# Branch A's engines in an order written by hand, three places for gate results, kept sums asked for later, and one sum of the early feed-forward moved ahead of weight sums

## The chip, the cores and the metric

One Trainium2 chip, of which the kernel uses one core. TensorE (PE, with PEld for its weight loads), VectorE (DVE), ScalarE (ACT) and GpSimd (POOL) each work through a queue of their own, in the order in which instructions stand in it; SyncE (SP) issues the DMAs, in the order of its queue. The metric is the device time of one execution in microseconds; a kernel's time is the median of its runs.

## The reference, cut to what matters

A hybrid encoder block over 1024 tokens and 16 meta tokens, width 1024, in float32: differential attention with 4 heads (branch A), windowed grouped attention (branch B), a sigmoid gate for each branch, an output projection, then a SwiGLU feed-forward of width 2816.

```python
def diff_attn_rows(q1, q2, k1, k2, v, qpos, kpos, key_real, slopes, lam):
    ...
    s1 = jnp.einsum('bqhd,bkhd->bhqk', q1, k1).astype(jnp.float32) * scale + bias
    s2 = jnp.einsum('bqhd,bkhd->bhqk', q2, k2).astype(jnp.float32) * scale + bias
    attn = jax.nn.softmax(s1, axis=-1) - lam * jax.nn.softmax(s2, axis=-1)
    return jnp.einsum('bhqk,bkhe->bqhe', attn.astype(v.dtype), v)

def mixer_block(...):
    ...
    merged = jax.nn.sigmoid(ga) * (y_a @ w_ba) + jax.nn.sigmoid(gb) * (y_b @ w_bb)
    return merged @ w_o

def swiglu(h, w_gate, w_up, w_down):
    return (jax.nn.silu(h @ w_gate) * (h @ w_up)) @ w_down
```

## The kernel before

Every large product runs as three products of split operands: a float32 operand is kept as a high part (rounded, written by ACT) and a low part (the difference, written by DVE or POOL), and high x high, high x low and low x high are summed in PSUM. The gates and the feed-forward also use a seven-product scheme on 2 x 2 blocks (products numbered 1 to 7), so that sums of weights and sums of activations are operands, and results of products are sums that are kept and added to later.

The program runs through these stages: the input projection and branch B's attention; **branch A with the gate products** (lines L738 to L893); the two branches' output weights (PE line L808, tiles ppa); the output projection; the feed-forward's gate and up products (L1466, tiles pg), whose first products are the "early feed-forward"; the down products (L1582).

**Branch A** goes through 4 heads of 8 query tiles each, 32 tiles, one round of the loop for each, and one round more, since tile n is scored while tile n-1 is transposed. The string `SLOTS` says in which order PE gets its work in a round: "s" is one block of scores (two matmuls of L829 into a bank, six blocks: three key blocks for softmax 1, then three for softmax 0), "g" one quarter of a gate product (three matmuls of L738), "t" one set of transposes of the tile before (L855), "n" a piece of values or of the head's norm (L868, L881, L891). Only PE's order is fixed by hand in the kernel before (`manual_schedule` for PE); ACT, DVE, POOL and SP have theirs set by the compiler's scheduler, which simulates a timeline.

For one tile, DVE takes each block of scores out of its bank and adds the distance bias with a running minimum (L832, six times), ACT takes the exponential of each softmax's row (L837, twice), DVE inverts the sum (L839), multiplies (L841) and joins the two softmaxes (L843, one pass over 1040 columns, "the join" below, with a short copy L844). PE transposes the joined tile in three pieces (L855); each piece leaves its bank as a high part by ACT (L858) and a low part by DVE (L859). Scores and transposes share five banks (`SC`).

The **gate products** fill PE between these blocks. `g_ahead` loads weights (L620) and splits them ahead (gop, hi by ACT, lo by POOL, L113 and L114). When a gate product's bank is complete, its result is either copied out by ACT (gate_stage, L746, two places: `G_BUFS`) or, for products 1, 6 and 7, added by DVE to a sum that was stored earlier and read back (gk, L743; read at L632 when the weights are split). Both are then stored (L747). Sums of w_o (tiles wo and wo_s, L774 to L786) are made by POOL between. The heads' Q and K are read at the head's first round (`load_a1`, `load_a0`), V with them (`load_v`).

**After the last gate product** come the branch B outputs: yb_raw is split into yb (hi by ACT, lo by DVE), w_b's first two weight blocks were read early (raw_w), the third is wbrb (L789).

**The early feed-forward** has DVE's order fixed by hand too. In it, product n is followed by what its results need (L1475 to L1486: a bank's sum with a stored copy, tile copies_p), by low parts of token sums (L1524, tile t, `low_of`), and `prepare()` makes the operands of a later product, for product 6 three sums of weights first (L1247 to L1249, tiles wf and s).

## Time and profile before

| | |
|---|---|
| three runs | 1453.79 us median (1452.72 to 1456.25) |
| the profiled execution's own time | 1453.61 us |
| its span | 1451.8 us |
| mean granted TensorE clock | 0.993 |
| PE from 324.8 to 638.4 us | branch A and the gate products |
| PE from 638.4 to 725.5 us | the branches' output weights |
| PE from 725.5 to 808.5 us | the output projection |
| PE from 808.5 to 1234 us | feed-forward, gate and up |
| PE from 1234 to 1444.8 us | feed-forward, down |

The columns of the views quoted below: a timeline row has start, duration, engine, line, operation, output<-inputs, shapes, the count of equal instructions in a row, and in brackets how long the engine had been idle before it and what released it. A row of windows has the stretch and its length, then busy time (and instructions) of PE, PEld, DVE, ACT and POOL, the granted clock, the DMA share and GB/s. A row of waits has the waiting line, what it waited for, the total, the number of times and the longest. A row of groups has the count, busy time, the mean in ns, and the idle time ahead of the group's instructions with its releasers.

### The profile page before, as it was taken

How to read it: one execution, taken by the hardware profiler on the slowest of the kernel's cores; microseconds unless marked ns; L12 is line 12 of the kernel's file. 1: busy time of each engine (PE TensorE's matmuls, PEld its weight loads, DVE VectorE, ACT ScalarE, POOL GpSimd, SP SyncE). 2: the span in 40 equal slices, each digit the busy share in tenths (PEclk: the TensorE clock that was granted, in tenths of full speed). 3: DMA queues.
4: the chain of work that ended last, by engine and by line, in shares of the span. 5: the costliest groups of instructions: out<-in, count | busy, mean ns of one | idle time of the engine just before them, and what ended most of it. 6: DMA issues, size and time to landing. Idle time of an engine off the chain costs nothing. (4 is left out here: it accounts for less than half of the span.)

```text
span 1451.8 us, 21189 instructions
## 1 busy us (share of the span) xinstructions
PE 1419.5 (98%) x7231; PEld 1216.4 (84%) x7231; DVE 943.4 (65%) x1680; ACT 696.0 (48%) x1315; POOL 627.2 (43%) x593
## 2 busy tenths in 40 slices
PE   8999999998999899999999999999999999999997
PEld 7998989987888889888888878888888888888886
DVE  7478535637778788733876896554455554787567
ACT  6366535545555455555445633333333333444454
POOL 4599126743532122245144565454445452000444
PEclk9999999999999999999999999999999999999999
DMA  8467668988768564569522624333333333964443
GB/s 242 88 210 239 191 164 269 277 287 290 250 221 257 175 196 155 167 209 330 201 80 88 189 87 150 119 109 105 100 96 107 103 103 105 316 223 139 124 130 139
DMA packets 195804, 255.00 MB, mean 176 GB/s; under 512 B 18976, under 2 KB 116704, under 8 KB 195696
## 3 DMA queue, kind: packets, MB, share of 16 engines
q1 hardware_dynamic: 195696, 253.65, 55.6%
q8 instruction: 57, 0.93, 0.3%
q14 instruction: 51, 0.42, 0.1%
HBM read 165.84 MB, written 81.20 MB: 170 GB/s over the span
## 5 line engine op out<-in xcount | busy, mean ns | idle before, releaser
L114 POOL TENSOR_TENSOR wop<-wf,wop 128x512 fp32r<-128x512 f32 x128 | 175.1, 1372 | 167.8 <-ACT wop L113 155.3
L1466 PE MATMUL pg<-t,wop 128*128 128x512 f32 x1056 | 242.6, 389 | 0.0
L1466 PEld LDWEIGHTS pg<-t,wop 128*128 128x128 f32 x1056 | 198.3, 188 | 41.1
L1582 PE MATMUL pd<-ob,oa 128*128 128x512 f32 x924 | 210.4, 389 | 0.5 <-POOL oa L114 0.4
L1582 PEld LDWEIGHTS pd<-ob,oa 128*128 128x128 f32 x924 | 173.2, 188 | 37.6 <-POOL oa L114 0.9
L1466 PE MATMUL pg<-b,wop 128*128 128x512 f32 x792 | 185.2, 392 | 2.8 <-DVE copies_p L1480 2.8
L1466 PEld LDWEIGHTS pg<-b,wop 128*128 128x128 f32 x792 | 149.5, 189 | 34.2 <-DVE copies_p L1480 3.2
L738 PE MATMUL pg<-hT_hi,gop 128*128 128x512 f32 x384 | 144.4, 400 | 0.4 <-DVE gk L743 0.4
L114 POOL TENSOR_TENSOR gop<-gr,gop 128x512 fp32r<-128x512 f32 x47 | 64.4, 1373 | 165.7 <-ACT gop L113 161.3
L113 ACT ACTIVATE wop<-wf 128x512 fp32r<-128x512 f32 x128 | 80.1, 631 | 84.1 <-PE pg L1466 48.0
L114 POOL TENSOR_TENSOR oa<-ra,oa 128x512 fp32r<-128x512 f32 x33 | 44.1, 1337 | 170.6 <-ACT oa L113 169.2
L113 ACT ACTIVATE oa<-ra 128x512 fp32r<-128x512 f32 x77 | 48.7, 632 | 105.1 <-PE pd L1582 44.0
L837 ACT ACTIVATE as<-as,amn 128x1040 f32<-128x1040 f32 x64 | 74.5, 1164 | 49.9 <-DVE amn L832 41.4
L829 PE MATMUL aps<-ak,aq 128*128 128x392 f32 (+1 forms) x384 | 91.0, 331 | 7.1 <-DVE amn L832 6.2
L1247 DVE TENSOR_TENSOR s<-wf,wf 128x512 f32<-128x512 f32 x22 | 22.3, 1011 | 103.4 <-DMA wf<-in_w_ff_up_dram 52.3
L829 PEld LDWEIGHTS aps<-ak,aq 128*128 128x128 f32 x384 | 70.4, 192 | 21.0 <-DVE amn L832 7.5
L738 PEld LDWEIGHTS pg<-hT_hi,gop 128*128 128x128 f32 x384 | 73.3, 191 | 12.2 <-DVE gk L743 1.1
L339 POOL TENSOR_SCALAR bs<-bs,bdn 128x432 f32<-128x432 f32 (+1 forms) x64 | 41.4, 664 | 86.6 <-DVE bdn L337 74.3
L738 PE MATMUL pg<-hT_lo,gop 128*128 128x512 f32 x192 | 76.5, 398 | 0.0
L114 POOL TENSOR_TENSOR woh<-wo,woh 128x512 fp32r<-128x512 f32 x28 | 38.5, 1378 | 67.4 <-ACT woh L113 66.3
L329 DVE CUSTOM_DVE_ANT_0 bs<-bps,tbx,nsink 128x432 f32<-128x432 f32 (+1 forms) x64 | 38.2, 622 | 38.5 <-PE bps L327 29.3
L832 DVE CUSTOM_DVE_ANT_0 as<-aps,dist,far_a 128x392 f32<-128x392 f32 x64 | 39.6, 619 | 30.2 <-PE aps L829 29.7
(311 smaller groups left out, 3219.2 us busy)
## 6 DMA issues: line engine op xcount, KB each, us to landing
ra<-aop SPq DMA_DIRECT2D x77, 256.0 KB, 2.7
wf<-in_w_ff_gate_dram SPq DMA_DIRECT2D x24, 512.0 KB, 4.0
wf<-in_w_ff_up_dram SPq DMA_DIRECT2D x24, 512.0 KB, 3.9
aop<-as SPq DMA_DIRECT2D x44, 256.0 KB, 2.1
w_c<-in_w_in_dram SPq DMA_DIRECT2D x17, 512.0 KB, 5.9
aop<-c SPq DMA_DIRECT2D x33, 256.0 KB, 2.0
ts_d<-to SPq DMA_DIRECT2D x16, 512.0 KB, 3.6
gw<-in_w_in_dram SPq DMA_DIRECT2D x32, 256.0 KB, 4.2
```

The lines of the kernel that those rows point to most:

```text
L113: nc.scalar.activation(hi, src, AF.Copy)
L114: lo_eng.tensor_tensor(lo, src, f32(hi), ALU.subtract)
L329: nc.vector.tensor_tensor_reduce(st[:, r, :W], ps[:, :W], tb, 2.0 ** -(4 * g + r + 1), nsink[:, 4 * g + r:4 * g + r + 1], ALU.add, ALU.min ...
L339: nc.gpsimd.tensor_scalar(st[:, r, :W], st[:, r, :W], dn[:, r:r + 1], 1.0, ALU.mult, ALU.mult)
L738: nc.tensor.matmul(ps, op[:, a, c], quad(b, *act)[:, c], start=(p in (2, 5, 1) and c == 0 and i == 0), stop=(p in (2, 3, 4) and c == 3 and ...
L829: nc.tensor.matmul(ps[:, :n], qs[m][:, t * P:(t + 1) * P], ks[m][:, vv, k0:k0 + n], start=(vv == 0), stop=(vv == 1))
L832: nc.vector.tensor_tensor_reduce(s[m][:, k0:k0 + n], ps[:, :n], far_by, slope, low, ALU.add, ALU.min, mn[:, m, i:i + 1])
L837: nc.scalar.activation(s[m][:, 0:L], s[m][:, 0:L], AF.Exp, bias=low, scale=-1.0, accum_out=sum_of[m])
L1247: tt(s1, a21, a22, ALU.add)
L1466: nc.tensor.matmul(ps, op[:, x, c, :], b[:, y, c, :], start=(p in (1, 2, 5) and c == 0 and n == 0), stop=(p in (4, 2, 3) and c == 3 and n ...
L1582: nc.tensor.matmul(ps[u], oa[:, a, u * P:(u + 1) * P], ob[:, b, :], start=(p in (1, 2, 5) and j == 0 and k == 0), stop=(p in (2, 3, 4) and ...
```

## The change

Six things change, five of them in branch A:

- ACT, DVE, POOL and SP get an order by hand over the whole loop of branch A. For that, `scores_a` is cut into the blocks themselves and `exp_a`, `scale_a`, `join_a`, which the loop calls at set places: the exponential of softmax 1 and the scale in the same round after the third and fifth block, the exponential of softmax 0 in the next round after the first set of transposes (`EXP_AT`), the join behind the next tile's first block (`JOIN_AT`). Weight splits are held back (`held_back`) and let go at two places of a round, or when a gate product needs them. A round's order for PE stays but for round 1, which gets two more "g" ("sgsgsngsgssggtntnt").
- A gate result is taken out not behind its own last matmul but after the next quarter's three matmuls (`owed`, `gate_result`).
- Gate results have three places instead of two, in another pool; the first uses a place of tag "w". yg has one buffer instead of two.
- Kept sums are no longer read when the weights are split but up to three ahead, at the second quarter of a gate product (`kept_to_do`, `load_kept`), which puts the read behind earlier stores in SP's queue.
- The next head's Q and K are asked for in the last tile of a head, right behind the blocks that used the old ones last; V in the third round of a head; the stores of w_o's sums in the round after they were made. `fill(1000)`, the last gate products, now stands ahead of the closing of the pools.
- In the early feed-forward `prepare()` is left out for products 4 to 7 and called behind product 7, and one of the token sums is made from the other bank's copy (one ACT copy and one DVE subtraction in the place of one DVE subtraction, four times).

```diff
-G_BUFS = 2
+JOIN_AT = 1
+EXP_AT = 1
+G_BUFS = 3
...
         if p in (1, 6, 7):
-            kept = g_kept[p, k] = gpool.tile([P, 512], F32, tag="gk", name=f"gk{p}_{k}", bufs=GK_BUFS)
-            nc.sync.dma_start(kept, g_place(p, k))
+            kept_to_do.append((p, k))
...
+    def load_kept():
+        p, k = kept_to_do.pop(0)
+        kept = g_kept[p, k] = gpool.tile([P, 512], F32, tag="gk", name=f"gk{p}_{k}", bufs=GK_BUFS)
+        nc.sync.dma_start(kept, g_place(p, k))
...
-                what(g_done[i])
+                if i and held_back is not None:
+                    held_back.append(g_done[i])
+                else:
+                    what(g_done[i])
                 g_done[i] += 1
+
+    def let_go(n):
+        while n > 0 and held_back:
+            g_split(held_back.pop(0))
+            n -= 1
...
+    owed = []
+
+    def gate_result(p, k, ps):
+        if p in (1, 6, 7):
+            while (p, k) not in g_kept:
+                load_kept()
+            st = g_kept.pop((p, k))
+            nc.vector.tensor_tensor(st, ps, st, ALU.add)
+        else:
+            tag, bufs = ("w", 2) if (p, k) == order_g[0] else ("g", G_BUFS)
+            st = prepool.tile([P, 512], F32, tag=tag, name=f"gate_stage{p}_{k}", bufs=bufs)
+            nc.scalar.copy(st, ps)
+        nc.sync.dma_start(g_place(p, k), st)
...
             for c in range(4):
...
+                while owed:
+                    gate_result(*owed.pop(0))
+                if c == 1:
+                    while kept_to_do and len(g_kept) < GK_BUFS:
+                        load_kept()
                 if c == 3:
...
+                    owed.append((p, k, ps))
+                    if n == len(order_g) - 1:
+                        gate_result(*owed.pop(0))
                 yield
...
+    order_av = tc.manual_schedule(engines={mybir.EngineType.Activation, mybir.EngineType.DVE, mybir.EngineType.Pool, mybir.EngineType.SP})
+    order_av.__enter__()
     for n in range(AH * NT + T_LAG):
...
-        for what in SLOTS:
-            if what == "s":
-                next(scoring, None)
-            elif what == "t":
-                next(turning, None)
+        if n < AH * NT and t == 2 and h:
+            vs[h] = load_v(h)
+        if n < AH * NT:
+            wo_store()
+            if t in (2, 3, 4, 5):
+                wo_load(4 * h + t - 2)
+        scored = turned = 0
+        if n == AH * NT:
+            join_a(tiles[n - 1][2])
+        for what in SLOTS if n != 1 else "sgsgsngsgssggtntnt":
+            if what == "s" and n < AH * NT:
+                next(scoring)
+                scored += 1
+                if scored == JOIN_AT and n:
+                    join_a(tiles[n - 1][2])
+                if scored == 3:
+                    exp_a(s, 1)
+                    if t == NT - 1 and h < AH - 1:
+                        ahead = load_a1(h + 1)
+                    let_go(1)
+                if scored == 4 and t in (3, 4, 5, 6):
+                    wo_ahead(4 * h + t - 3)
+                if scored == 5:
+                    scale_a(t, s)
+                if scored == 6 and n == 0:
+                    exp_a(s, 0)
+                if scored == 6 and t == NT - 1 and h < AH - 1:
+                    ahead = load_a0(h + 1, *ahead)
+            elif what == "t" and n:
+                next(turning)
+                turned += 1
+                if turned == EXP_AT and n < AH * NT:
+                    exp_a(s, 0)
+                if turned == 3:
+                    let_go(1)
             elif what == "n":
                 step_tail()
-            else:
+            elif what == "g":
                 fill(1)
...
+    order_av.__exit__(None, None, None)
     n_gates[0] += HOLD
     raw_w = []
     while tail:
         step_tail()
+        let_go(9)
         fill(3)
...
     order_pe.__exit__(None, None, None)
+    fill(1000)
     close_pre()
...
-    fill(1000)
     ypool, close_ypool = pool("ypool")
...
-        nc.vector.tensor_tensor(left, t2, left, ALU.subtract)
+        nc.scalar.copy(left, pts[1])
+        nc.vector.tensor_tensor(left, left, pts[0], ALU.subtract)
...
-        if n not in (4, 5):
+        if n not in range(4, 8):
             prepare()
...
         product_f(*steps[n][1])
         used[0] -= 1
+        if n == 7:
+            prepare()
         low_of(2)
```

Three places show how instructions move. The first is ACT's queue around rounds 2 to 4 of branch A: at is the high part of a transposed piece, "as...<-as,amn 128x1040" an exponential (with adn as its sum, it is softmax 1), gop a weight split, gate_stage a gate result. Before:

```order
L837 ACTIVATE as_0_3180,as_0_0_3937<-as_0_3180,amn_2_4064 128x1040
L837 ACTIVATE as_0_3_4141,adn_3_4140<-as_0_3_4141,amn_3_4139 128x1040
L746 COPY gate_stage<-pg_0_4003 128x512
L113 ACTIVATE gop_2_4251<-gr_2_4146 128x512
L858 ACTIVATE at_2_4063<-apt_2_0_4200 128x4x128
L837 ACTIVATE as_1_3181,as_0_0_3937<-as_1_3181,amn_3_4139 128x1040
L858 ACTIVATE at_2_4063<-apt_2_1_4216 128x4x128
L858 ACTIVATE at_2_4063<-apt_2_2_4230 128x128
```

and now:

```order
L115 ACTIVATE gop_3_4147<-gr_3_4038 128x512
L885 ACTIVATE as_0_3_4154,adn_3_4153<-as_0_3_4154,amn_3_4152 128x1040
L756 COPY gate_stage_0_4192<-pg_0_3997 128x512
L909 ACTIVATE at_2_4072<-apt_2_0_4212 128x4x128
L885 ACTIVATE as_1_3181,as_0_0_3934<-as_1_3181,amn_3_4152 128x1040
L909 ACTIVATE at_2_4072<-apt_2_1_4229 128x4x128
L909 ACTIVATE at_2_4072<-apt_2_2_4243 128x128
L115 ACTIVATE gop_2_4247<-gr_2_4104 128x512
L885 ACTIVATE as_0_4_4257,adn_4_4256<-as_0_4_4257,amn_4_4254 128x1040
```

The split stands behind the transposed pieces instead of ahead of them, and softmax 0's exponential always stands between a tile's first and second transposed piece.

The second place is ACT's queue at the end of the gate products: yb is a high part of branch B's output, wbhb of its weights, gate_stage the copies of the last two gate results. Before:

```order
L113 ACTIVATE yb_7340<-yb_raw_6945 128x512
L113 ACTIVATE yb_7341<-yb_raw_6945 128x512
L113 ACTIVATE gop_6_7198<-gr_6_7171 128x512
L113 ACTIVATE gop_7_7228<-gr_7_7196 128x512
L113 ACTIVATE wbhb_7306<-raw_w_7207 128x512
L113 ACTIVATE wbhb_7309<-raw_w_7208 128x512
L746 COPY gate_stage<-pg_6_7084 128x512
L746 COPY gate_stage<-pg_7_7140 128x512
L113 ACTIVATE wbhb_7446<-wbrb_7362 128x512
```

and now:

```order
L115 ACTIVATE gop_6_7221<-gr_6_7171 128x512
L115 ACTIVATE gop_7_7235<-gr_7_7196 128x512
L115 ACTIVATE wbhb_7310<-raw_w_7208 128x512
L115 ACTIVATE wbhb_7313<-raw_w_7209 128x512
L756 COPY gate_stage_6_7285<-pg_6_7065 128x512
L756 COPY gate_stage_7_7298<-pg_7_7133 128x512
L115 ACTIVATE wbhb_7450<-wbrb_7366 128x512
L115 ACTIVATE yb_7342<-yb_raw_6947 128x512
L115 ACTIVATE yb_7343<-yb_raw_6947 128x512
```

The splits of yb, eight in all, stood ahead of the last weight splits and now stand behind the last gate result and behind the third weight block of branch B.

The third is DVE's queue in the early feed-forward: c and copies_p are sums with banks, t low parts of token sums, s and wf sums of weights. Before:

```order
L1475 TENSOR_TENSOR c_1_11_9074<-pg_1_2_9061,copies_p_0_0_8945 128x512
L1524 TENSOR_TENSOR t_8913<-ts_8894,t_8913 128x4x128
L1524 TENSOR_TENSOR t_8912<-ts_8984,t_8912 128x4x128
L1247 TENSOR_TENSOR s_0_0_6_9088<-wf_0_0_9084,wf_0_1_9086 128x512
L1248 TENSOR_TENSOR wf_0_0_9084<-wf_0_0_9084 128x4x128
L1249 TENSOR_TENSOR wf_0_0_9084<-s_0_0_6_9088,wf_0_0_9084 128x4x128
L1247 TENSOR_TENSOR s_1_0_6_9099<-wf_0_0_9095,wf_0_1_9097 128x512
L1248 TENSOR_TENSOR wf_0_0_9095<-wf_0_0_9095 128x4x128
L1249 TENSOR_TENSOR wf_0_0_9095<-s_1_0_6_9099,wf_0_0_9095 128x4x128
L1524 TENSOR_TENSOR t_8912<-ts_9040,t_8912 128x4x128
L1524 TENSOR_TENSOR t_8913<-ts_8984,t_8913 128x4x128
L1480 TENSOR_TENSOR copies_p_0_0_8945<-pg_1_2_9127,copies_p_0_0_8945 128x512
```

and now:

```order
L1552 TENSOR_TENSOR c_1_11_9082<-pg_1_2_9069,copies_p_0_0_8951 128x512
L1601 TENSOR_TENSOR t_8919<-ts_8899,t_8919 128x4x128
L1601 TENSOR_TENSOR t_8918<-ts_8990,t_8918 128x4x128
L1601 TENSOR_TENSOR t_8918<-ts_9047,t_8918 128x4x128
L1601 TENSOR_TENSOR t_8919<-ts_8990,t_8919 128x4x128
L1557 TENSOR_TENSOR copies_p_0_0_8951<-pg_1_2_9107,copies_p_0_0_8951 128x512
L1559 TENSOR_TENSOR c_1_11_9082<-c_1_11_9082,copies_p_0_0_8951 128x512
L1323 TENSOR_TENSOR s_0_0_6_9129<-wf_0_0_9125,wf_0_1_9127 128x512
L1324 TENSOR_TENSOR wf_0_0_9125<-wf_0_0_9125 128x4x128
L1325 TENSOR_TENSOR wf_0_0_9125<-s_0_0_6_9129,wf_0_0_9125 128x4x128
```

The bank's sum (copies_p) and the product with it moved ahead of the six sums of weights; the same count of instructions stands there.

70 lines of the change are left out of this document (35 added, 35 removed).

## The prediction

> **What bounds the kernel now.** First the page: the engines' busy time and shares of the span.
>
> ```profile
> PE 1419.5 (98%) x7231; PEld 1216.4 (84%) x7231; DVE 943.4 (65%) x1680; ACT 696.0 (48%) x1315; POOL 627.2 (43%) x593
> ```
>
> PE is busy for 98% of the span and the change neither adds nor removes a matmul: time can only come from PE's gaps and from its clock. So the next view is the windows, for the changed stage, for three stretches of one head's rounds each (heads 1, 2 and 3), and for the early feed-forward's changed place.
>
> ```profile
> 324.80:638.40 313.60, 298.79 (x1769) 266.68 (x1768) 239.41 (x664) 173.21 (x324) 97.68 (x77) 0.98 0.64 210
> 416.18:452.58 36.40, 36.40 (x238) 33.77 (x237) 33.35 (x98) 24.33 (x48) 7.75 (x8) 1.00 0.56 187
> 489.56:526.27 36.71, 36.57 (x238) 33.76 (x237) 33.13 (x99) 22.73 (x44) 7.61 (x7) 1.00 0.39 127
> 557.55:601.30 43.75, 42.31 (x262) 37.98 (x260) 41.37 (x115) 25.77 (x48) 11.13 (x9) 1.00 0.39 125
> 840.50:848.00 7.50, 4.77 (x14) 3.83 (x15) 7.50 (x8) 3.18 (x6) 6.16 (x5) 0.77 0.09 35
> ```
>
> In branch A PE is idle for 313.60 - 298.79 = 14.8 us, and its clock stood at 0.98: 2% of 313.6 is 6.3 us. So 21.1 us is the most that the stage can give. Inside a head PE has next to none of it: in the second row its busy time equals the stretch. But DVE stands close behind: 33.4 of 36.4 us there, 41.4 of 43.75 in head 3. The waits of PE in the stage say where the 14.8 us are.
>
> ```profile
> PE aps L829 <- DVE amn L832: 6.2, 4, 2.2
> PE apt L855 <- DVE as L843: 4.4, 5, 2.0
> PE apf L891 <- POOL af L886: 1.5, 1, 1.5
> PE apt L855 <- DVE amn L832: 1.2, 2, 0.6
> PE aps L829 <- DMA ak<-ka_d: 0.9, 1, 0.9
> ```
>
> They name DVE, yet DVE waits itself. The timeline shows for what, at the start, at the first change of heads and at the second:
>
> ```profile
> 336.24 0.16 DVE L839 RECIPROCAL adn<-adn 128x1 f32<-128x1 f32 x1 [4.48 <-ACT as L837]
> 337.05 0.62 PE L829 MATMUL aps<-ak,aq 128*128 128x392 f32 x2 [1.65 <-DVE amn L832]
> 340.94 1.81 PE L855 MATMUL apt<-ident,as 128*128 128x128 f32 x9 [1.98 <-DVE as L843]
> 403.38 0.59 ACT L746 COPY gate_stage<-pg 128x512 f32<-128x512 f32 x1 [3.46 <-DMA g_d<-gate_stage]
> 405.96 0.81 PE L829 MATMUL aps<-ak,aq 128*128 128x392 f32 x2 [2.15 <-DVE amn L832]
> 475.02 0.69 DVE L743 TENSOR_TENSOR gk<-pg,gk 128x512 f32<-128x512 f32 x1 [4.86 <-DMA gk<-g_d]
> 479.27 0.69 DVE L743 TENSOR_TENSOR gk<-pg,gk 128x512 f32<-128x512 f32 x1 [2.18 <-DMA gk<-g_d]
> 480.42 0.62 PE L829 MATMUL aps<-ak,aq 128*128 128x392 f32 x2 [1.96 <-DVE amn L832]
> 386.90 0.65 PE L891 MATMUL apf<-ident,af 128*128 128x128 f32 x4 [1.47 <-POOL af L886]
> ```
>
> At the start the inverse of the first sum came 4.48 us late, since ACT's exponential stood behind weight splits that waited for loads; PE lost 1.65, then 1.98 to the first join. At 403.38 ACT had stood 3.46 us before a gate copy, which found both places still being stored, and the exponential behind it was late: 2.15 on PE. At 475 and 479 DVE stood 4.86 and 2.18 us before sums that were read back too late; PE lost four pieces there, the largest 1.96. With the norm's 1.47 these are the gaps of near 2 us. Behind such a gap matmuls run slower: the 340.94 row has 9 transposes in 1.81 us, and 12 matmuls take 4.56 us behind 2.76 us of idling in the feed-forward, against 2.89 before it:
>
> ```profile
> 817.65 2.89 PE L1466 MATMUL pg<-b,wop 128*128 128x512 f32 x12
> 836.10 0.68 DVE L1247 TENSOR_TENSOR s<-wf,wf 128x512 f32<-128x512 f32 x1
> 841.29 1.28 DVE L1524 TENSOR_TENSOR t<-ts,t 128x512 fp32r<-128x512 f32 x2
> 842.49 0.68 DVE L1480 TENSOR_TENSOR copies_p<-pg,copies_p 128x512 f32<-128x512 f32 x1
> 843.23 4.56 PE L1466 MATMUL pg<-b,wop 128*128 128x512 f32 x12 [2.76 <-DVE copies_p L1480]
> ```
>
> So that gap costs 2.76 + 1.67 = 4.4 us; the granted clock was 0.77 in the 840.5 row. The Trainium skill ("TensorE: Matmul & The Clock Gate", Part 1: The HAM clock gate) has half rate begin only after an idle window of about 3.4 us; the trace disagrees, with slow matmuls behind 2.76 us and 1.98 us, and the measurement decides. By the rule only the idle 14.8 us could be won in branch A, and the estimate would be some 6 us worse.
>
> **The change part by part, against the profiled execution's 1453.61 us** (0.18 below the median).
>
> *Start, changes of heads, kept sums, norm.* The exponential now stands ahead of the splits, round 1 has two more gate quarters to cover the first join, results have three places, the kept sums come up to three ahead, and Q and K are asked for behind their last reader. The idle time with a named cause is 1.65 + 1.98 at the start, 2.15 at the first change, 0.86 + 0.53 + 0.45 + 1.96 = 3.8 at the second (from the PE rows between 470 and 481), 1.47 at the norm: 11.05 us. The 6.3 us of clock go with these, since only gaps of this size are followed by slow matmuls. That makes 17.35. Against all of it speaks SP's queue:
>
> ```profile
> SPq L632 <- DMA g_d<-gk: 29.0, 20, 2.9
> ```
>
> A kept sum's read waits in SP's queue until its store has landed, up to 2.9 us, and everything behind it on SP (weights, stores of results, now the next head's K) waits too. Up to three reads now stand together, so I leave one gap of 2 us in: **-15.4** (bounds: -17.35 and, if the heads' ends stay as they are, -7.6).
>
> *The rest of the idle time,* 14.8 - 11.05 = 3.75 us, is small waits for the join in the heads in which DVE is nearly full. What the new order does to them is read from ACT's and DVE's durations:
>
> ```profile
> L837 ACT ACTIVATE as<-as,amn 128x1040 f32<-128x1040 f32 x64 | 74.5, 1164 | 49.9 <-DVE amn L832 41.4 <-DVE as L844 7.8
> L858 ACT ACTIVATE at<-apt 128x512 fp32r<-128x512 f32 x64 | 37.2, 587 | 18.5 <-PE apt L855 18.4
> L859 DVE TENSOR_TENSOR at<-apt,at 128x512 fp32r<-128x512 f32 x64 | 43.3, 685 | 6.9 <-ACT at L858 6.7
> L843 DVE SCALAR_TENSOR_TENSOR as<-as,adn,as 128x1040 f32<-128x1040 f32 x32 | 43.2, 1350 | 0.5
> L743 DVE TENSOR_TENSOR gk<-pg,gk 128x512 f32<-128x512 f32 x24 | 16.4, 683 | 12.0 <-DMA gk<-g_d 7.0 <-PE pg L738 4.7
> ```
>
> The exponential of softmax 0 now stands between a tile's first two transposed pieces. While DVE works off the first low part (0.685), ACT needs 1.164 + 0.587 for the exponential and the second high part: DVE, when it is the later engine, waits 1.07 us in each round. PE needs 36.4 us for five rounds here, 7.3 a round; DVE 33.35 / 5 = 6.7, with the wait 7.7. Over a head of eight rounds that is an excess of some 3 us, which the five score banks and the first round's gate quarters (ten, 0.7 us each) absorb in part. In heads 0 and 1, with few gk additions, I lay the rounds out to no stall; in heads 2 and 3, 24 additions of 0.683 come on top, and a layout by these durations leaves 2.7 us a head. So 3.75 becomes 5.4: **+1.7** (bounds -3.75, if DVE never is the later one, and the slower rival's).
>
> *Gate results behind the next quarter* put three matmuls, 0.7 us, ahead of each copy; with three places that lies beside PE's work and costs nothing unless the banks run out. w_o's stores a round later, V in the third round and one yg go by the same argument: their readers are rounds away, and what hides them is the round's own 7 us. Without that cover a late V would stop PE once a head, for about the 2 to 3 us of a load.
>
> *The end of the gate products.* Here a wait is added. What stands there now:
>
> ```profile
> 621.53 4.27 ACT L113 ACTIVATE yb<-yb_raw 128x512 fp32r<-128x512 f32 x8
> 622.19 1.29 DVE L114 TENSOR_TENSOR yb<-yb_raw,yb 128x512 fp32r<-128x512 f32 x2 [1.87 <-ACT yb L113]
> 626.48 2.35 DVE L114 TENSOR_TENSOR yb<-yb_raw,yb 128x512 fp32r<-128x512 f32 x2
> 638.41 9.93 PE L808 MATMUL ppa<-yb,wbhb 128*128 128x512 f32 x43
> 638.61 0.38 SPq L789 DMA_DIRECT2D wbrb<-in_w_branch_b_dram  x1
> 641.54 0.63 ACT L113 ACTIVATE wbhb<-wbrb 128x512 fp32r<-128x512 f32 x1 [2.35 <-DMA wbrb<-in_w_branch_b_dram]
> ```
>
> The eight splits of yb ran at 621.5 to 625.8, below gate products, and PE went over into L808 at 638.41 without a gap. In the new order they are behind the last gate copy and behind the split of the third weight block, which SP only asks for once the last gate matmul has freed its place (638.61) and which reached ACT at 641.54, 2.93 later. All that time the first product of L808 waits for its yb. Its first high part is done at 641.54 + about 0.55 (the step between ACT's splits, 4.27 / 8) + 0.63 = 642.7: 4.3 us of gap. Its low part takes DVE another 0.62 to 1.2 (the two DVE rows), part of it beside matmuls, and the slow clock behind a gap of this size cost 1.67 at 843.23. From 4.3 (nothing else shows) to 4.3 + 1.2 + 1.67 = 7.2; I take the gap with most of one clock's loss, **+5.5**. Nothing later gives it back, because the ppa stage is PE's own.
>
> *Early feed-forward.* The bank's sum ran at 842.49 behind six sums of weights (836.10 to 841.29) and two low parts. Now four low parts stand ahead of it, two of them (1.28 together) from behind the sums: 836.10 + 1.3 = 837.4 to 838, ahead of 840.47, when PE came to need it. The gap goes, 4.4 us. Late next are the weight operands, since the sums now end 0.7 to 1.4 us later and `prepare()` runs behind product 7: by the rows the first operand is ready at about 843.5 to 844, needed at 843.5 when PE has not stopped, so 0 to 2 us come back. The four ACT copies stand where ACT is idle and DVE's count is the same. **-4.0** (bounds -4.4 and -2.4).
>
> Sum: -15.4 + 1.7 + 5.5 - 4.0 = -12.2, 1441.4; to the median +0.2, so **1442 us**.
>
> **The rivals.**
>
> 1. *All gaps go and DVE is never late:* -17.35 - 3.75 + 4.3 - 4.4 = -21.2, **about 1433**. For it: PE's rounds without a gap in head 1. Against: DVE's 95% in head 3 (41.37 of 43.75).
>
> 2. *The changes of heads stay late,* because the next K stands in SP's one queue behind kept sums that wait for stores (29.0 us over 20 waits): only the start, 3.63 with about 2.5 of clock, and the norm are won: -7.6 + 1.7 + 5.5 - 4.0 = -4.4, **about 1449**. Against: K's room is free a few us earlier now.
>
> 3. *Slower: DVE becomes the bound in branch A.* Place: the wait of 1.07 between the first and the second low part, in every round. On top the join gets longer when POOL works beside it:
>
> ```profile
> 345.74 1.30 DVE L843 SCALAR_TENSOR_TENSOR as<-as,adn,as 128x1040 f32<-128x1040 f32 x1
> 353.43 1.93 DVE L843 SCALAR_TENSOR_TENSOR as<-as,adn,as 128x1040 f32<-128x1040 f32 x1
> 352.97 1.29 POOL L785 TENSOR_TENSOR wo_s<-wo,wo_s 128x512 f32<-128x512 f32 x1
> ```
>
> The hand-made order lets splits go at fixed places, and a split's POOL part may fall on the join each time: 0.6 more a round. 1.07 + 0.6 against the slack of 7.3 - 6.7 = 0.6 leaves 1.1 in each of 32 rounds, 35 us, less what four heads' first rounds absorb (2 to 2.5 us each): +26. Then 1453.6 - 15.4 + 26 + 5.5 - 4 = **about 1466**. It decides against the change when the excess per round passes some 0.75 us. The Trainium skill ("SBUF — State Buffer", Terms) gives VectorE and GpSimd a shared port pair that the loser waits for; these rows agree, 0.63 us on the join, and by that rule every such meeting costs it. Against it: DVE's wait only counts where DVE is the later engine, and PE runs ahead by several banks.
>
> 4. *The early feed-forward does not gain,* with the operand of product 6 as late as the sum was: 4 us more, 1446, within the forecast's own range.
>
> **How the numbers follow.** The forecast (1437 to 1447, with the fourth case) 0.47; rival 1 0.2; rival 2 0.2; rival 3 0.13. A measurement of this kernel tells 0.3%, 4.4 us, from no change: faster is below 1449.4, slower above 1458.2. The forecast and rival 1 are faster, and not half of rival 2; rival 3 is mostly slower, its lower part within: 0.75 faster, 0.13 within, 0.12 slower. The range takes rival 1's end and rival 2 with a part of the third: 1432 to 1455; the likeliest case's own is 1437 to 1447.
>
> **What would show it.** Right: PE's stretch of branch A about 299 to 304 us long at a clock of 1.00; no idle time of ACT before a gate copy by a DMA and none of several us on DVE before gk; a PE row of L808's successor with about 4 us of idle time behind ACT yb or DVE yb, and a clock below 1 behind it; no PE wait for copies_p near 840. Wrong: PE waits for amn or for the join that recur in every round with DVE full (rival 3), PE waits for ak at 400, 471 and 545 (rival 2), no gap at the first product of L808 (then 5 us better), or a wait for a weight operand near 843 that is as long as the old one.

## The result, and the profile after

| | before | after |
|---|---|---|
| median | 1454.22 us (4 runs, 1452.72 to 1456.25) | 1504.18 us (4 runs, 1502.34 to 1505.58) |
| ratio, 95% interval | | 1.0342 (1.0324 to 1.0360): slower |
| span of the profiled execution | 1451.8 us | 1502.6 us |
| mean granted clock | 0.993 | 0.980 |

The forecast was 1442 us, with a range from 1432 to 1455. The time was 50 us above the kernel before, on the side of the third rival and beyond its price. Where the 50.8 us of the two spans lie, read from PE's first and last instruction of each stage:

| stage on PE | before | after | difference |
|---|---|---|---|
| up to the first gate product of branch A | 324.8 | 323.2 | -1.6 |
| branch A, first to last gate matmul | 313.8 | 357.6 | +43.8 |
| last gate matmul to the end of the branch weights | 87.1 | 95.1 | +8.0 |
| to the first product of the feed-forward | 82.9 | 84.6 | +1.7 |
| gate and up products | 425.5 | 424.0 | -1.5 |
| down products and the rest | 217.7 | 218.2 | +0.5 |

The page's busy time of the changed kernel, and then two rows of its windows (stretch, length, busy time of PE, PEld, DVE, ACT and POOL, clock, DMA share and GB/s), branch A in the first:

```profile
PE 1441.0 (96%) x7231; PEld 1232.0 (82%) x7231; DVE 953.7 (63%) x1680; ACT 692.7 (46%) x1319; POOL 629.2 (42%) x593
```

```profile
324.60:680.30 355.70, 318.92 (x1762) 281.86 (x1761) 244.65 (x656) 163.18 (x314) 100.69 (x77) 0.93 0.57 184
680.30:780.00 99.70, 93.65 (x399) 76.31 (x399) 56.80 (x81) 52.22 (x88) 33.14 (x26) 0.97 0.73 237
```

PE is idle for 355.70 - 318.92 = 36.8 us, where it was 14.8, and its clock is 0.93 instead of 0.98. So of the 42.1 us by which this window is longer than before's (313.60), idling is 22.0, and 20.1 are busy time of PE (318.92 against 298.79), though its matmuls are the same ones. The clock accounts for some 18.6 of these, an estimate from the two rounded clocks (7% of 355.7 less 2% of 313.6). Two more rows show how: the 6.8 us behind one of PE's gaps, and the 6.8 us after them.

```profile
431.90:438.70 6.80, 6.80 (x25) 6.22 (x26) 4.38 (x11) 3.25 (x7) 1.68 (x2) 0.50 0.45 154
438.70:445.50 6.80, 6.80 (x46) 6.31 (x46) 5.12 (x18) 4.76 (x9) 2.54 (x2) 1.00 0.12 41
```

PE is busy all the time in both, but gets through 25 matmuls at a clock of 0.50 and 46 at 1.00.

DVE is busy for no more than 244.65 of 355.7 us: over the stage it is nothing like full. The waits of PE from 324 to 720 us, and under them those of DVE and ACT (what waited, for what; total, times, longest):

```profile
PE apst L932 <- ACT ysq L926: 15.1, 7, 2.3
PE apt L906 <- DVE amn L875: 13.9, 13, 2.1
PE ppa L850 <- ACT yb L115: 4.4, 1, 4.4
PE aps L872 <- DMA ak<-ka_d: 2.8, 3, 1.2
...
DVE at L910 <- ACT at L909: 46.5, 54, 3.3
...
ACT as L885 <- DVE amn L875: 143.6, 38, 10.5
```

Each engine waits for the next: PE for ACT's ysq and, at the transposes, for a bank that DVE's score blocks behind the join must free, DVE 46.5 us for ACT's high parts, ACT 143.6 us for DVE's blocks. (In the kernel before the last two were 6.7 and 41.4 us, by the prediction's rows of L859 and L837.) It is a circle of waits, with neither DVE nor ACT full. One round shows it, in the timeline of the changed kernel:

```profile
422.59 0.58 ACT L909 ACTIVATE at<-apt 128x512 fp32r<-128x512 f32 x1
423.07 1.16 ACT L885 ACTIVATE as<-as,amn 128x1040 f32<-128x1040 f32 x1
424.22 0.75 ACT L909 ACTIVATE at<-apt 128x512 fp32r<-128x512 f32 x2
424.83 0.88 DVE L910 TENSOR_TENSOR at<-apt,at 128x512 fp32r<-128x512 f32 x2 [0.94 <-ACT at L909]
426.47 1.49 DVE L894 SCALAR_TENSOR_TENSOR as<-as,adn,as 128x1040 f32<-128x1040 f32 x1
428.09 0.62 DVE L875 CUSTOM_DVE_ANT_0 as<-aps,dist,amn 128x392 f32<-128x392 f32 x1
429.45 1.16 ACT L885 ACTIVATE as<-as,amn 128x1040 f32<-128x1040 f32 x1 [3.49 <-DVE amn L875]
431.13 0.57 ACT L926 ACTIVATE ysq<-apy 128x512 f32<-128x512 f32 x1
423.25 1.08 PE L919 MATMUL apy<-at,av 128*128 128x256 f32 x7
425.32 0.52 PE L872 MATMUL aps<-ak,aq 128*128 128x392 f32 x2
431.75 1.79 PE L932 MATMUL apst<-ones,ysq 128*128 128x1 f32 x8 [2.19 <-ACT ysq L926]
```

ACT does the first high part, then the exponential, then the other high parts; DVE stands still 0.94 us before its second low part. So it comes to the join at 426.47 and to the second block of the next tile at 428.09, although PE had filled that block's bank at 425.32 + 0.52 = 425.8. The exponential of softmax 1 needs the third of these blocks and starts at 429.45, after 3.49 us of idling on ACT. Behind it, by the order by hand, stands ysq. Its input, the values, had been complete since 423.25 + 1.08 = 424.3; it ran at 431.13, and PE stood 2.19 us for it.

### The profile page after: what moved, and what is told of

Same layout as the page of the kernel before. It is cut to its first block, busy times and chain, and to the rows that moved or that the text cites. A ratio compares the mean times of both kernels' runs of the same rounds, so it can differ in the third digit from the quotient of the medians.

```text
span 1502.6 us, 21144 instructions
## 1 busy us (share of the span) xinstructions
PE 1441.0 (96%) x7231; PEld 1232.0 (82%) x7231; DVE 953.7 (63%) x1680; ACT 692.7 (46%) x1319; POOL 629.2 (42%) x593
## 5 line engine op out<-in xcount | busy, mean ns | idle before, releaser
L116 POOL TENSOR_TENSOR gop<-gr,gop 128x512 fp32r<-128x512 f32 x47 | 60.5, 1286 | 231.6 <-ACT gop L115 211.1
L773 PE MATMUL pg<-hT_hi,gop 128*128 128x512 f32 x384 | 150.4, 416 | 3.1 <-ACT gop L115 2.5
L885 ACT ACTIVATE as<-as,amn 128x1040 f32<-128x1040 f32 x64 | 74.4, 1163 | 143.7 <-DVE amn L875 143.6
L115 ACT ACTIVATE wop<-wf 128x512 fp32r<-128x512 f32 x128 | 80.3, 630 | 87.1 <-PE pg L1543 47.8
L872 PE MATMUL aps<-ak,aq 128*128 128x392 f32 (+1 forms) x384 | 97.2, 350 | 4.6 <-DMA ak<-ka_d 2.8
L872 PEld LDWEIGHTS aps<-ak,aq 128*128 128x128 f32 x384 | 75.4, 205 | 19.5 <-issue 2.3
L773 PEld LDWEIGHTS pg<-hT_hi,gop 128*128 128x128 f32 x384 | 77.0, 201 | 16.0 <-ACT gop L115 2.7
L910 DVE TENSOR_TENSOR at<-apt,at 128x512 fp32r<-128x512 f32 (+1 forms) x96 | 50.2, 550 | 47.0 <-ACT at L909 46.5
L341 POOL TENSOR_SCALAR bs<-bs,bdn 128x432 f32<-128x432 f32 (+1 forms) x64 | 41.4, 667 | 85.4 <-DVE bdn L339 74.1
L906 PE MATMUL apt<-ident,as 128*128 128x128 f32 x288 | 49.0, 292 | 13.9 <-DVE amn L875 13.9
```

The source lines that it names most:

```text
L115: nc.scalar.activation(hi, src, AF.Copy)
L116: lo_eng.tensor_tensor(lo, src, f32(hi), ALU.subtract)
L341: nc.gpsimd.tensor_scalar(st[:, r, :W], st[:, r, :W], dn[:, r:r + 1], 1.0, ALU.mult, ALU.mult)
L773: nc.tensor.matmul(ps, op[:, a, c], quad(b, *act)[:, c], start=(p in (2, 5, 1) and c == 0 and i == 0), stop=(p in (2, 3, 4) and c == 3 and ...
L872: nc.tensor.matmul(ps[:, :n], qs[m][:, t * P:(t + 1) * P], ks[m][:, vv, k0:k0 + n], start=(vv == 0), stop=(vv == 1))
L885: nc.scalar.activation(s[m][:, 0:L], s[m][:, 0:L], AF.Exp, bias=s["low", m], scale=-1.0, accum_out=sum_of[m])
```

## The experiments

Each ran beside the kernel before on the same chip. "Branch A" is again the stretch from the first to the last gate matmul of the profiled execution; the kernel before has 313.8, the changed one 357.6.

| run | median us | ratio to before (95%) | branch A us |
|---|---|---|---|
| e1 ysq a step earlier | 1500.5 | 1.0318 (1.0291 to 1.0346) | 356.5 |
| e2 exponential behind the pieces | 1494.8 | 1.0264 (1.0230 to 1.0299) | 339.1 |
| e3 last results in another pool | 1498.1 | 1.0298 (1.0274 to 1.0322) | 358.4 |
| e4 feed-forward part undone | 1502.7 | 1.0327 (1.0300 to 1.0354) | 357.6 |
| e5 scheduler's order in branch A | 1459.1 | 1.0049 (1.0030 to 1.0067) | 306.6 |
| e6 e2 and splits off the join | 1480.2 | 1.0182 (1.0157 to 1.0208) | 334.8 |
| e7 five repairs | 1469.8 | 1.0119 (1.0091 to 1.0147) | 328.4 |
| e8 before with the feed-forward's order | 1450.6 | 0.9984 (0.9969 to 0.9998) | 315.9 |
| e9 ACT free | 1489.7 | 1.0261 (1.0232 to 1.0289) | 343.5 |
| e10 DVE free | 1482.9 | 1.0214 (1.0190 to 1.0239) | 333.9 |
| e11 SP and POOL alone by hand | 1462.5 | 1.0069 (1.0047 to 1.0092) | 313.2 |
| e12 e5, e3 and e4 | 1449.1 | 0.9976 (0.9959 to 0.9994) | 310.5 |
| e13 e10 and e1 | 1464.4 | 1.0085 (1.0052 to 1.0118) | 314.7 |
| e14 e9 and low parts between blocks | 1475.3 | 1.0159 (1.0120 to 1.0198) | 324.8 |
| e15 order by hand, repaired | 1461.0 | 1.0057 (1.0039 to 1.0076) | 323.6 |

### First: one repair at a time

**e1.** The norm's first ACT step is joined to the last piece of values.

```diff
-            yield
+            if part < 2:
+                yield
...
             yield from normed_a(h, t // 4, acc[0])
+        else:
+            yield
```

> The changed kernel, but the norm's first two ACT instructions (ysq, yg) are issued one step earlier, right behind the last values matmuls, so that in ACT's queue they stand ahead of the next tile's first exponential. Theory (PE's wait apst <- ACT ysq, 15.1 us in 7 gaps of up to 2.3, comes from ysq standing in ACT's queue behind an exponential that itself waits for a block on DVE): the wait falls below 2 us, most of the slow clock behind these gaps goes too, and the time is 1504 less 15 to 27, that is 1477 to 1489. Rival (DVE is late in every round, and PE only loses the same time at the next place): the wait goes to the join and to free score banks, and the time stays above 1496.

PE's waits in branch A:

```profile
PE aps L872 <- DVE amn L875: 15.0, 25, 1.5
PE apt L906 <- DVE amn L875: 10.1, 10, 1.8
```

The wait for ysq is gone (15.1 us to nothing) and the stretch is 1.1 us shorter. The rival was right: score banks are waited for 15.0 us in 25 pieces instead of 1.4 in 3. As long as DVE is late in each round, taking away another wait only lets PE reach DVE's sooner. The clock of the window did recover, from 0.93 to 0.97, and still PE's busy time came down by no more than 1.9 us (to 316.98); the trace does not show apart where that gain went.

**e2.**

```diff
-EXP_AT = 1
+EXP_AT = 3
```

> The changed kernel, but the exponential of softmax 0 is issued behind all three transposed pieces instead of behind the first. Theory (DVE stands still for the second high part, at <- ACT at, 46.5 us in 54 waits, since ACT does the exponential between the first two): that wait falls below 20 us, PE's waits for the join (13.9 us) fall below 5, the time falls by 15 to 30, to 1474 to 1489. Rival (the exponential is needed for the join just as soon, so DVE stands still there instead): a new DVE wait for ACT's exponential of 15 us or more, and a time within 5 us of 1504.

DVE's wait for high parts fell from 46.5 to 24.2 us, PE's at the transposes from 13.9 to 7.6, branch A by 18.5; the median fell by 9, the profiled execution by 17. The theory's direction holds, its size only in part. What was left showed in the timeline of e2, with POOL under DVE:

```profile
525.98 2.19 DVE L894 SCALAR_TENSOR_TENSOR as<-as,adn,as 128x1040 f32<-128x1040 f32 x1
528.20 1.15 DVE L895 COPY as<-as 128x32 f32<-128x32 f32 x1
525.79 1.29 POOL L116 TENSOR_TENSOR gop<-gr,gop 128x512 fp32r<-128x512 f32 x1 [4.49 <-ACT gop L115]
527.03 2.29 POOL L820 TENSOR_TENSOR wo_s<-wo_s,wo 128x512 f32<-128x512 f32 x1
```

The join takes 2.19 us and its copy 1.15 while POOL works, since a split is let go at the same place of each round.

**e3.** The last two results take a place of tag "gr" in gpool.

```diff
+            if (p, k) in order_g[-2:]:
+                st = gpool.tile([P, 512], F32, tag="gr", name=f"gate_stage{p}_{k}", bufs=GR_BUFS)
+            else:
```

> The changed kernel, but the last two gate results are copied into the pool of gate weights instead of the pool whose memory the split of yb takes over. Theory (the yb splits stand behind the last gate copy because their memory is the closed pool's, so the order is forced): the splits move back below the gate products, the first product of L850 follows the last gate matmul with no gap, and the time falls by 4.4 idle + 0.6 + about 2.3 of slow clock, 7 us, to about 1497. Rival (PE must wait there in any case, for weights): the gap stays at 4 us with another releaser, time 1504.

The stretch behind the last gate matmul fell from 95.1 to 87.1 us, what it was before the change, and the first ppa matmul follows with no gap. So what tied ACT's order there was that pool: with the last results out of prepool, the splits went back below the gate products.

**e4.** `prepare()` and the token sum as before the change.

> The changed kernel with the whole early feed-forward part undone (order of operands and the sum from a copy as before). Theory (that part took away one gap of 4.4 us with its slow clock and put three in its place, 1.16 + 1.75 + 0.73 us, before sums that now wait for ACT copies): the time stays within 2.5 us of 1504. Rival (the part gained its 4 us, as forecast, and the loss lies in branch A alone): 1508 or more.

The time stayed (1502.7 against 1504.2): as a whole the feed-forward's part was worth nothing that stands out of the runs' spread (1501.7 to 1505.6 for both kernels together). Why, e8 shows.

**e8.** The kernel before, with the token sum left to DVE and this:

```diff
-        if n not in (4, 5):
+        if n not in range(4, 8):
             prepare()
...
+        if n == 7:
+            prepare()
```

> The kernel before with the feed-forward part of the change alone, but the token sum still made by DVE from its own sum, without ACT's copy. Theory (the moved sum takes the gap at 840 us away, and only the ACT copies gave it back): no PE wait for copies_p, faster by 3 to 4.4 us, about 1450. Rival (weight operands behind the moved sums are late instead): a new wait near 843 and the time within 1.5 us of before.

Neither came true as written. The gap went from its place and came back at the next sum of a bank, the time is 1.7 us lower at the medians (interval 0.0 to 0.3%). The products of the kernel before up to its gap, then the places where PE stood in the changed kernel, then in e8:

```profile
821.17 19.30 PE L1466 MATMUL pg<-b,wop 128*128 128x512 f32 x84
```

```profile
860.45 5.74 PE L1543 MATMUL pg<-b,wop 128*128 128x512 f32 x24 [1.16 <-ACT kept L1433]
875.14 22.00 PE L1543 MATMUL pg<-b,wop 128*128 128x512 f32 x96 [1.75 <-DVE kept L1434]
906.03 8.45 PE L1543 MATMUL pg<-t,wop 128*128 128x512 f32 x36 [0.73 <-DVE copies_p L1557]
874.31 0.69 DVE L1434 TENSOR_TENSOR kept<-kept,ptn_f 128x512 f32<-128x512 f32 x1 [2.10 <-ACT kept L1433]
```

```profile
822.91 22.02 PE L1466 MATMUL pg<-b,wop 128*128 128x512 f32 x96
856.08 10.06 PE L1466 MATMUL pg<-t,wop 128*128 128x512 f32 x36 [2.63 <-DVE copies_p L1480]
839.07 0.68 DVE L1480 TENSOR_TENSOR copies_p<-pg,copies_p 128x512 f32<-128x512 f32 x1
851.98 3.44 DVE L1253 TENSOR_TENSOR wf<-wf,wf 128x512 f32<-128x512 f32 x2
855.35 0.68 DVE L1480 TENSOR_TENSOR copies_p<-pg,copies_p 128x512 f32<-128x512 f32 x1
```

In both, 96 products run where the kernel before broke off after 84. In e8 the next sum of a bank (855.35) is late by 2.63 us, nearly the old 2.76, 36 products on: DVE works from 828 to 857 without a pause, and what is moved behind one sum stands in front of the next. In the changed kernel ACT's copy adds two stops of its own, 1.16 and 1.75 us, and the later sum is late by only 0.73, PE itself having been held up before it.

### Second: the order by hand as a whole, and two engines apart

**e5, e9, e10, e11** change the set of engines in `manual_schedule` over branch A: none, then DVE, POOL and SP, then ACT, POOL and SP, then SP and POOL.

```diff
-    order_av = tc.manual_schedule(engines={mybir.EngineType.Activation, mybir.EngineType.DVE, mybir.EngineType.Pool, mybir.EngineType.SP})
+    order_av = tc.manual_schedule(engines={mybir.EngineType.DVE, mybir.EngineType.Pool, mybir.EngineType.SP})
```

> The changed kernel without the hand order of ACT, DVE, POOL and SP in branch A: the compiler's scheduler sets them as before, everything else of the change stays (three places, results behind the next quarter, kept sums later, Q, K and V asked for earlier or later, the end of the gate products, the feed-forward). Theory (the hand order alone is what branch A loses by): PE's stretch of branch A falls from 356 to 316 us or less, and the time to 1457 to 1466, where the stall at the end of the gate products is left. Rival (the other parts, late results and late reads above all, cost a good part): 1475 or more, with PE waits for gk, for free gate banks or for K.

> The changed kernel with the hand order for DVE, POOL and SP alone; ACT's order is the scheduler's. Theory (the loss comes from ACT's queue: the exponential between two pieces, splits and ysq at set places): within 8 us of e5's 1459. Rival (DVE's own fixed order keeps it late, since it has nothing else to do while it waits for ACT): 1480 or more, with DVE idle before at for 20 us or more. A third: both share it, 1468 to 1480.

> The changed kernel with the hand order for ACT, POOL and SP alone; DVE's order is the scheduler's. Theory of ACT's queue: 1485 or more. Rival (DVE's fixed order): within 8 us of e5's 1459, since DVE takes score blocks while it waits for the exponential. Both: 1468 to 1485.

> The changed kernel with the hand order for SP and POOL alone. Every theory that puts the loss on ACT's and DVE's orders expects e5's time within 6 us, 1453 to 1465. If SP's one queue with late reads, or POOL's fixed order, is what costs: 1470 or more, with PE or DVE waits that end on a DMA.

e5 settles the larger part: without the order by hand 45 of the 50 us are gone, and branch A takes 306.6 us in its profile, 7 fewer than before the change (the profiled execution, 1452.2, was the fastest of ten that reach to 1465). With SP and POOL by hand (e11) it takes 313.2, and the time is in the range that was expected if ACT's and DVE's orders are what costs. Between these two, e9 ended where the rival had it and e10 in the range for "both". PE's waits in e9 and e10 divide the loss:

```profile
PE apt L906 <- DVE amn L875: 16.6, 15, 2.7
PE aps L872 <- DVE amn L875: 6.9, 11, 3.0
```

```profile
PE apst L932 <- ACT ysq L926: 15.1, 7, 2.9
...
PE apt L906 <- DVE amn L875: 1.2, 1, 1.2
```

With ACT free, ysq is no longer waited for, but DVE's blocks are, for 23.5 us. With DVE free the wait for blocks at the transposes falls to 1.2, and ysq's stays at 15.1. There are two faults, one in each queue; freeing one engine wins 14.1 (e9) or 23.7 us (e10) of branch A, freeing both (e11) 44.4, which is 6.6 more than the sum: each hides a part of the other, as e13 shows below.

**e6 and e7.** In e6 the splits are let go in one place:

```diff
-                    let_go(1)
+                    let_go(2)
...
-                if turned == 3:
-                    let_go(1)
```

e7 takes e1, e3 and e6 together, with the token sum made as before.

> e2 (exponential behind the three pieces) with the second weight split of a round let go together with the first, behind the exponential of softmax 1, so that POOL's part no longer starts with the join. Theory (POOL beside the join is the second half of DVE's lateness: joins of 2.2 us and copies of 1.1 us where 1.3 and 0.2 do it alone): the mean of the join falls from 1420 to about 1330 ns, that of its copy from 639 below 300, PE's waits for the join below 4 us, time 1477 to 1487. Rival (the collision only moves to other DVE work or is hidden): within 4 us of e2's 1495.

> The changed kernel with all the repairs at once: exponential behind the pieces, splits off the join, ysq and yg a step earlier, the last two gate results in the other pool, and the token sum of the feed-forward made without ACT's copy. Theory (each stall has its own place in a queue, and together they leave DVE enough room in each round): apst waits below 2 us, no gap at the end of the gate products, branch A below 325 us, time 1450 to 1464. Rival (the fixed order of DVE keeps it late by more than five score banks can hold, whatever the rest does): branch A above 333 us, time above 1468.

DVE's groups in e6 (mean ns behind the busy time):

```profile
L894 DVE SCALAR_TENSOR_TENSOR as<-as,adn,as 128x1040 f32<-128x1040 f32 x32 | 41.6, 1301 | 1.1
L895 DVE COPY as<-as 128x32 f32<-128x32 f32 x32 | 5.8, 181 | 1.1
```

The join's mean fell from 1420 ns in e2 to 1301 and the copy's from 639 to 181, as expected. The gain lies between 4.3 us (branch A of the profiled executions) and 14.6 (medians; e2's runs reach from 1487 to 1496). In branch A PE's waits at the transposes fell from 7.6 to 1.5 us, but those for the next head's K rose from 1.2 to 6.4. e7 ended on the rival's side in time (above 1468) and between the two in branch A, 328.4 us, with 6.2 us of waits for the next head's K among them: the repairs help together, and something is left.

### Third: the two faults by themselves

> e10 (DVE's order by the scheduler, ACT, POOL and SP by hand) with ysq and yg a step earlier, as in e1. Theory (with DVE no longer late, ysq's place in ACT's queue is the whole of what the hand order still costs; in e1 it was hidden behind DVE's lateness): the 15.1 us wait of apst goes below 3 and the time falls from 1483 by 18 to 26, to 1457 to 1465. Rival (as in e1, the loss only moves to another wait): above 1474.

> e9 (ACT's order by the scheduler, DVE, POOL and SP by hand), but DVE's second and third low part of a tile are issued behind the next tile's first and second score block, and the join behind them. Theory (DVE stands still before a low part although score blocks are ready, and that makes PE wait for banks): DVE's wait for ACT before at falls from 25 to below 10 us, PE's waits for amn from 23.5 to below 10, time from 1490 to 1466 to 1478. Rival (the join as such comes too late for PE, whatever DVE does before it): within 5 us of 1490.

**e13** is e10 with e1's edit. Branch A fell by 19.2 us and the median by 18.5, where the same edit gave 1.1 and 3.7 in e1: with DVE not late, ysq's place was nearly all that ACT's order still cost (314.7 us against e11's 313.2). **e14** is e9 with this:

```diff
-            nc.vector.tensor_tensor(lo, pt[:lo.shape[0], :nb], f32(hi)[:lo.shape[0]], ALU.subtract)
+            late_lo.append((lo, pt[:lo.shape[0], :nb], f32(hi)[:lo.shape[0]]))
+            if b == 0:
+                low_now(1)
             yield
...
                 scored += 1
+                if scored < 3:
+                    low_now(1)
```

with the join behind the second block (`JOIN_AT = 2`). DVE's wait for high parts fell from 25.0 to 10.7 us, PE's for blocks at these two lines from 23.5 to 7.7, branch A by 18.7, the time by 14.4, in the theory's range. New are 3.0 us of PE's waits for the join at the transposes and 2.6 for blocks at the norm. Score blocks that lie ready fill the time in which ACT makes the next high part. The low parts and the join moved together here, so the share of each is not shown.

**e15** has all four engines by hand, with e7's places, e14's low parts and the feed-forward part undone.

> All four engines by hand, with every repair: e7's places of the exponential, the splits, ysq and the last gate results, e14's low parts between score blocks, and the feed-forward part undone. Theory (the order itself, not that it is fixed by hand, is what costs): branch A at 306 to 318 us and 1448 to 1458. Rival (a fixed order cannot follow rounds of two lengths): 1462 or more.

At 1461.0 it lies between the two expectations. The repairs took back 43 us (from 1504.2), 8 of them at the end of the gate products, so that the order is fixed by hand was not the chief cause; but the ratio is still 1.0057, and 17 us of branch A against e5's profile are left. PE's longest wait there is of another kind:

```profile
PE aps L875 <- DMA ak<-ka_d: 8.4, 6, 2.2
```

The rest of these 17 us was not followed up and stays open.

**e12** joins the useful parts: the scheduler's order (e5), the last results in the other pool (e3), the feed-forward as before.

> e5 (scheduler's order in branch A) with the last two gate results in the other pool, as in e3, and the feed-forward part undone: what is left of the change is the earlier or later loads, three places and results behind the next quarter. Theory (branch A gains by these, the stall at its end goes): branch A 306 us as in e5's profile instead of 314, no gap before the branch weights, 1447 to 1451, faster than both. Rival (e5's runs spread from 1452 to 1465, since the late reads leave no slack against loads): 1452 to 1456, no better than before.

1449.1 us over 12 runs, 4 us below the kernel before at the medians, ratio 0.9976 (0.9959 to 0.9994): a quarter of a per cent faster than the kernel before, and the lowest median here. Its interval overlaps that of e8 (0.9969 to 0.9998), so which of these two is the faster is open. Branch A was 310.5 in its profile and not 306, with one wait of 4.1 us for a gate copy; the runs spread from 1442.6 to 1455.6.

## Why the prediction was wrong

- **The bound and the gaps of before** were read rightly in the main: PE's 14.8 us of idling and some 5 to 6 of clock were the whole that could be won in branch A. (The 6.3 came of a clock rounded to 0.98; the trace has three stretches of 3.4 us at a clock of 0.50, from 341, 406 and 481 us, which make 5.1.) e5, without the order by hand, won 7.2 of them in its profile.
- **The term that failed is "+1.7" for the rest of the idle time.** The pause on DVE behind the exponential was seen and priced at 1.07 us a round; the changed trace has 0.94 in the round shown. The mistake is the step from there: five rounds were averaged to 7.3 us of PE against 7.7 of DVE, and the banks were said to absorb the difference in heads 0 and 1. The sum had 5.4 us of waits left; measured were 13.9 at the transposes alone: 6.55 in five rounds of head 0, which was laid out to no stall, none in head 1, and 7.38 in heads 2 and 3. DVE's fixed order belongs to the cause: in e10, with ACT's order as it was and DVE's left to the scheduler, these waits are 1.2 us. Why the banks absorbed so little was read from the traces only, no run varied it. Rounds come in two lengths, 5.7 and 8.6 us for the fifth and sixth of the kernel before, which had no stall there (8.6 and 10.3 in the changed kernel), and five banks are less than one round. 9.5 of the 13.9 us stand in the short rounds, those without values, in which DVE's chain (low parts, block, join, block) has the least room.
- **ysq was not in the prediction at all.** The queue of ACT was read for the exponential and the splits, not for what the norm has behind them: 15.1 us, with the slow clock behind each of the seven gaps.
- **The clock** was counted as a gain of 6.3; it became a loss, some 24.9 us (7% of 355.7), since gaps of 1.8 us and more came nine times instead of three, seven of them ysq's. In branch A the two terms, -15.4 and +1.7, forecast 13.7 us less, and it took 43.8 more. Of the 57.5 between them the clock is about 25, ysq 15.1, the transposes 8.5 (13.9 for 5.4), PE's other waits 5.8 (7.8 where 2 were left in); some 3 are not assigned. These shares are estimates from the figures above.
- **The third rival** had the main mechanism, DVE late through the exponential (e2, e14), and the wrong size: 1466. It subtracted 2 to 2.5 us a head for what the banks absorb and knew nothing of ysq. Its name was wrong too: DVE is not full (244.65 of 355.7), it stands still. Of its second part, POOL on the join, the place was right and the price was not: in 17 of the 32 rounds a split's POOL part did meet the join, and made it 1.48 us instead of 1.30 (the 426.47 row), not 0.6 longer. Nor does every such meeting cost the join: in the kernel before, the one at 582.50 took 1.29 us, with POOL's instruction beginning 0.39 us after it. Join and copy together took 0.17 us a round more than before in the changed kernel (means of 1396 and 420 ns, 1350 and 295 before) and 0.41 more in e2.
- **Start and changes of heads, "-15.4":** under the scheduler's order (e5) the gaps at the norm and at the second change of heads went but for about 1 us. At the first change 1.7 us of waits, 1.4 of them for K, stood where 2.15 had been. The first tile's stayed (5.3 us lost in the second round, 4.5 before). In the order by hand the start lost about 3 us in the third round instead. A late V cost PE nothing, though its load took 5.6 us and not the 2 to 3 of the prediction.
- **The end of the gate products, "+5.5":** right in place and cause, gap 4.35 for a forecast 4.3. With the second gap of 0.59 and the slow clock it is 8.0, a little beyond the bound of 7.2; e3 takes it back whole. The rows:

```profile
683.91 0.63 ACT L115 ACTIVATE wbhb<-wbrb 128x512 fp32r<-128x512 f32 x1 [2.53 <-DMA wbrb<-in_w_branch_b_dram]
684.45 4.25 ACT L115 ACTIVATE yb<-yb_raw 128x512 fp32r<-128x512 f32 x8
685.11 0.80 PE L850 MATMUL ppa<-yb,wbhb 128*128 128x512 f32 x1 [4.35 <-ACT yb L115]
686.50 5.69 PE L850 MATMUL ppa<-yb,wbhb 128*128 128x512 f32 x14 [0.59 <-DVE yb L116]
```

- **The early feed-forward, "-4.0":** the old gap went, as forecast, and nothing was won (e4). Two steps failed. "ACT copies stand where ACT is idle" left out that DVE waits for them (2.10 us before L1434). And "late next are the weight operands" was wrong: the next bank's sum was late (e8).

## What to carry to other kernels

Judge an order by hand by each engine's stretch from one hand-over to the next in the shortest round, not by means over rounds: here buffers of less than a round carried little from long rounds to short ones. In a queue, put work that is ready between two steps that wait for another engine, and never put a result that PE asks for soon behind an instruction that waits for a later one. When several waits form a circle, one repair alone may show nothing (e1: 1 us of branch A; the same edit gave 19 once DVE was on time), so free whole engines first to see where the loss lies.

## What the runs showed that was not expected

The slow matmuls behind a gap are not a fixed price. Three kernels stood for 2.8 us at the same sum of the early feed-forward, and its next 12 products took 4.56 us in the kernel before (row 843.23 of the prediction), 4.23 in e12 and 3.03 in e4:

```profile
839.27 4.23 PE L1542 MATMUL pg<-b,wop 128*128 128x512 f32 x12 [2.77 <-DVE copies_p L1556]
```

```profile
894.20 3.03 PE L1542 MATMUL pg<-b,wop 128*128 128x512 f32 x12 [2.80 <-DVE copies_p L1556]
```

The last is 0.25 us a product, hardly slowed: the clock was 1.00 from 894.2 to 897.2, where the kernel before had 0.51 from 843.2 to 846.6. Behind 1.75 us (the 875.14 row above) 96 products took 22.00, 0.23 each, not slowed at all. The Trainium skill ("TensorE: Matmul & The Clock Gate", Part 1: The HAM clock gate) has the clock decided over a window that runs freely and does not begin with the gap; that gaps of equal length differ agrees with it, that 2.8 us is at times enough does not agree with its window of about 3.4 us.

POOL's share in DVE's lateness was larger than on the join alone: the copy of 32 columns behind it took 1.15 us beside POOL in e2 and 181 ns on the mean where no POOL work met it in e6.
